# New cost numbers for the list scheduler that orders a Gated DeltaNet layer's front

## The chip, the cores and the metric

The kernel runs on one core of a Trainium2 chip. The core has TensorE for matrix products (PE in the profile, its weight loads PEld), VectorE (DVE), ScalarE (ACT), GpSimd (POOL), SyncE (SP), which here issues the transfers, and 16 DMA engines behind a hardware queue. Each engine works through its own list of instructions in order, and semaphores connect the lists. The metric is device time in microseconds of one execution, the median of several runs.

## The reference

One layer of a diffusion backbone in fp32: a bidirectional gated DeltaNet over 512 latent tokens with a prefix of 256 context tokens, width 1024, 8 heads of 128, then a mixture of 16 experts with expert-choice routing. Both are fed by RMSNorm and modulation (shift, scale, gate) that is computed from `c`. Cut to what matters here:

```
mod = silu(c) @ w_mod + b_mod                    # 6 x 1024 columns: shift, scale, gate of both parts
u = modulate(rmsnorm(x), shift, scale)           # latent and context tokens
q, k, v = silu(short_conv(u @ w_in, width 5)); z = u @ w_z
decay g and beta from u; l2norm of q and k
for both directions, for each head, in chunks of 64 tokens:
    L = I + strict_lower((beta k) k^T * decay)   # 64 x 64, unit lower triangular
    u_vals, w_keys = solve(L, [beta v, beta k exp(gcum)])
    scan over chunks:  v_new = u - w S;  o = q_dec S + att v_new;  S = g S + k_tail^T v_new
y = (rmsnorm(o) * gain * silu(z)) @ w_out
x = x + gate * y
then: 16 experts, each takes its best tokens; out = x + gate * sum(p * (silu(h Wg) * (h Wu)) Wd)
```

## The kernel before

The kernel has a **front** (norms, projections, eight heads, output projection, router) and then a **loop over the experts**, which gathers tokens by a one-hot matmul (L1511, tile `gc`) and multiplies them with the experts' weights (L1561, L1580). Those weights, tiles `w`, come in transfers of 1 to 2 MB that SP issues (L636) as soon as buffers are free, the first of them while the front still runs.

A product in fp32 is made of three matmuls on split operands: `wh` and `uh` are the rounded halves, `wl` and `ul` the remainders (L141 to L143 for the projections, L457 to L459 for the output projection, "a triple" below). ACT rounds, and DVE or POOL subtracts (L299 and L303 for the projections' weights, loaded as `wt` on L136; L733 and L735 for the output weights).

**The heads.** Each head q goes through steps that follow on one another:

- convolutions of its projected columns (L283, DVE);
- part A, `head_a`: two loads `ff` of the decay rows (L1060, from `grow_d`), a mask on POOL (L1065), exponentials on ACT, products into `ct` and `cd` on DVE (L1116 to L1125), and `cd` goes to DRAM (`bd`, L1128);
- the inversion of the triangular blocks: `lb` comes back from `bd` in another layout (L1137), POOL works 62 alternating steps on 96 partitions (L1148 `tb`, L1150 `xb`), and the result goes out as `xd` (L1153) and returns as `cr` (L1158);
- part B, `head_b`: from `cx` (L1217, DVE) to the transposed inverse `XT` (L1277, L1278);
- the scan over chunks in two directions (L1302 to L1352: `R` L1318, `Vs` L1326, `vx` L1330, the state L1337), with a decayed query `qa`, which is loaded (L1290), exponentiated on ACT and multiplied on POOL (L1298);
- norm and gating, transposes on PE (L1382), the head's output `ot` (L1385).

**The modulations.** 32 pieces of 512 KB (`mods` and `mod_piece`, L338 to L398) yield shift, scale and gate columns that are needed late. A string names the engine of each piece; a piece on DVE is 8 operations (L373, L375), then one matmul (L396) and one addition (L398). Loads are planned 7 us apart from 50 us on, into two buffers. The last eight pieces are the columns of the gate row `gtm`.

**The output projection.** `out_w` scales a piece of the output weights with `gtm` on POOL (L723; the code makes it wait for all eight columns), rounds it (L733) and subtracts (L735). Pieces come through a ring of three buffers `wot` (L716). Then 64 triples in five groups of heads, (0,1), (2,3), (4,5), (6) and (7), go to PE, and DVE adds each result to `hres` (L475). L766 splits the heads' outputs. The router follows: transposes L537, logits L514, L524, and L578.

**What sets the order.** Nothing of the front is written in the order in which it is issued. Every step is a Python generator that yields `Ask(engine, duration, earliest time, slot)` in front of each operation, and `run` (L213 to L237) is a greedy list scheduler: it keeps a planned time at which each engine is free, takes the step that can start first, or within a window (`LOOK`) one of better rank on the same engine, emits its instruction, and moves the planned time on by the duration. The result of a step counts as available after its duration and the hand-over `HOP` of its engine, or 0.06 us on the same engine. `dma` plans transfers as one queue with a rate and a latency. `RANK` is 1 for the scan and part A, 4 for part B, 5 and 6 for output, 7 for mods and convolutions. So the numbers in the `Ask`s decide in which sequence each engine's list is written; on the chip the lists run in order, as their semaphores allow.

## Time and profile before

| | us |
|---|---|
| median of three runs | 1574.02 (1568.37 to 1576.02) |
| the profiled execution | 1573.24 |
| its span | 1571.5 |
| PE, DVE, ACT, POOL busy | 1374.7, 721.5, 405.3, 381.0 |
| first gather of the expert loop | 633.51 |

The profile gives, for one execution, what each engine did at which time. A row of the timeline is an operation (or several alike): its start, its duration, engine, line, result and operands, and in brackets how long the engine had been idle and what ended the wait. A row of the groups sums operations of one line and shape. A row of the waits sums the idle time of an engine by what it waited for. A row of the windows shows how long each engine worked in a stretch of time, the granted share of TensorE's full clock, the busy share of the DMA engines and what they moved.

### The profile page before, as it was taken

Reading aid. Unit: us, or ns where it says so; the run is one execution under the profiler, and the core shown is the slowest. Engines: PE = TensorE matmul, PEld = TensorE weight load, DVE = VectorE, ACT = ScalarE, POOL = GpSimd, SP = SyncE. Lnnn points to the kernel's source line nnn. Section 1 sums busy time; section 2 is a strip of 40 time slices with the busy share of each in tenths; the row PEclk is TensorE's granted clock in tenths of the full one; section 3 lists DMA queues with packets and bytes.
Section 4 is the critical chain, followed back from the end, with each engine's and each line's share of the span. In section 5 each row is a group of like instructions: output and inputs, shape, how many; then the busy total and the mean of one; then the engine's idle time right before and its main releaser. Section 6 shows DMA issues by size and latency. Waiting matters only on the chain.

```text
span 1571.5 us, 20699 instructions
## 1 busy us (share of the span) xinstructions
PE 1374.7 (87%) x8058; PEld 752.6 (48%) x8058; DVE 721.5 (46%) x1545; ACT 405.3 (26%) x1038; POOL 381.0 (24%) x645
## 2 busy tenths in 40 slices
PE   5889898988986889999999989889889899899867
PEld 1677687766875766433434324224223323324314
DVE  7779896977995896222222222222222222222103
ACT  3356474655574533000000000000000000000012
POOL 2548866857657830000000000000000000000001
PEclk8889999999998999999999999999999999999979
DMA  8145443443453566899999999999999999999992
GB/s 347 54 135 142 135 114 91 117 130 95 133 122 72 205 243 248 364 426 426 425 426 425 425 426 426 427 425 425 426 425 426 426 425 426 425 426 426 425 426 109
DMA packets 112515, 480.12 MB, mean 306 GB/s; under 512 B 45505, under 2 KB 66209, under 8 KB 81826
## 3 DMA queue, kind: packets, MB, share of 16 engines
q1 hardware_dynamic: 112418, 478.81, 77.9%
q8 instruction: 63, 1.03, 0.3%
q14 instruction: 34, 0.28, 0.1%
HBM read 471.92 MB, written 6.86 MB: 305 GB/s over the span
## 4 chain that ended last, share of the span: by engine, by line
DMA 48%; PE 26%; DVE 14%; POOL 8%; issue 2%; ACT 1%; SPq 0%; DVEq 0%; POOLq 0%; ACTq 0%
DMA w<-in_wgu 25%; DMA w<-in_wd 13%; PE gu L1580 10%; PE dn L1561 4%; POOL xb L1150 3%; POOL tb L1148 3%; DMA cr<-xd 2%; DVE e L375 2%; PE gc L1561 2%; PE gc L1511 2%; DMA fg<-in_fg 1%; DVE wl L303 1%; DMA ff__690<-grow_d 1%; DMA ff__1139<-grow_d 1%; PE gc L1548 1%
## 5 line engine op out<-in xcount | busy, mean ns | idle before, releaser
L1580 PE MATMUL gu<-w,xsT 128*64 128x512 f32 x2044 | 472.9, 606 | 32.4 <-DMA w<-in_wgu 31.6
L1580 PEld LDWEIGHTS gu<-w,xsT 128*64 128x64 f32 x2044 | 138.4, 138 | 291.5 <-issue 239.4
L1667 POOL TENSOR_TENSOR hres<-acc,fg 128x256 f32<-128x256 f32 (+1 forms) x6 | 6.0, 1004 | 953.1 <-DVE acc L1655 953.0
L1561 PE MATMUL dn<-w,work 128*64 128x512 f32 x896 | 202.0, 600 | 25.2 <-DMA w<-in_wd 25.2
L1550 DVE TENSOR_TENSOR acc<-gc,acc 128x512 f32<-128x512 f32 x104 | 70.7, 690 | 299.5 <-PE gc L1548 299.5
L141 PE MATMUL pp<-uh,wh 128*128 128x512 f32 (+1 forms) x368 | 153.4, 417 | 1.7 <-ACT cz L265 1.7
L143 PE MATMUL pp<-uh,wl 128*128 128x512 f32 (+1 forms) x368 | 138.9, 377 | 3.8 <-DVE wl L303 2.9
L142 PE MATMUL pp<-ul,wh 128*128 128x512 f32 (+1 forms) x368 | 137.9, 375 | 0.0
L1561 PEld LDWEIGHTS dn<-w,work 128*64 128x64 f32 x896 | 62.4, 137 | 154.2 <-issue 116.8
L1148 POOL TENSOR_TENSOR tb<-lb,xb 96x126 f32<-96x126 f32 (+22 forms) x248 | 118.3, 477 | 65.8 <-DMA lb<-bd 48.6
L1150 POOL TENSOR_TENSOR xb<-xb,tb 96x126 f32<-96x126 f32 (+22 forms) x248 | 125.1, 504 | 19.4
L1532 ACT ACTIVATE work<-tr 128x512 f32<-128x512 f32 x14 | 8.4, 597 | 423.1 <-PE tr L1525 423.1
L1512 DVE TENSOR_SCALAR xsT<-gc,ffn 128x128 f32<-128x128 f32 x64 | 26.2, 410 | 154.1 <-PE gc L1511 154.1
L1542 ACT CAST yh<-work 64x512 fp32r<-64x512 f32 x28 | 17.3, 617 | 253.1 <-DVE work L1539 252.8
L143 PEld LDWEIGHTS pp<-uh,wl 128*128 128x128 f32 x368 | 74.7, 203 | 16.1 <-DVE wl L303 3.3
L141 PEld LDWEIGHTS pp<-uh,wh 128*128 128x128 f32 x368 | 75.1, 204 | 10.7 <-ACT cz L265 2.2
L142 PEld LDWEIGHTS pp<-ul,wh 128*128 128x128 f32 x368 | 75.3, 205 | 6.3
L1511 PEld LDWEIGHTS gc<-oneh,hres 128*128 128x128 f32 x512 | 64.5, 191 | 20.2 <-issue 18.3
L1511 PE MATMUL gc<-oneh,hres 128*128 128x128 f32 x512 | 69.2, 280 | 0.4 <-DVE oneh L1504 0.4
L375 DVE SCALAR_TENSOR_TENSOR e<-e,cs,e 128x128 f32<-128x128 f32 x133 | 66.0, 512 | 1.8
L1613 DVE TENSOR_TENSOR work<-gu,work 128x512 f32<-128x512 f32 x32 | 22.0, 692 | 80.9 <-PE gu L1580 79.7
L1548 PEld LDWEIGHTS gc<-yh,pgt 128*128 128x128 f32 x112 | 19.8, 186 | 82.0 <-issue 68.2
(443 smaller groups left out, 2042.7 us busy)
## 6 DMA issues: line engine op xcount, KB each, us to landing
w<-in_wgu SPq DMA_DIRECT2D x100, 2048.0 KB, 34.3
w<-in_wd SPq DMA_DIRECT2D x45, 2048.0 KB, 34.3
w<-in_wgu SPq DMA_DIRECT2D x55, 1024.0 KB, 31.9
w<-in_wd SPq DMA_DIRECT2D x22, 1024.0 KB, 31.8
e<-in_wm SPq DMA_DIRECT2D x32, 512.0 KB, 4.4
wt<-in_win SPq DMA_DIRECT2D x31, 512.0 KB, 4.6
w<-in_wdt SPq DMA_DIRECT2D x6, 2048.0 KB, 30.7
wm<-in_wm SPq DMA_DIRECT2D x3, 2048.0 KB, 14.6
```

Of the source, the lines that this page charges most:

```text
L141: pe.matmul(pp, wh[:, k, :], uh[i][:, k, :], start=k == 0, stop=False)
L142: pe.matmul(pp, wh[:, k, :], ul[i][:, k, :], start=False, stop=False)
L143: pe.matmul(pp, wl[:, k, :], uh[i][:, k, :], start=False, stop=k == KT - 1)
L375: v.scalar_tensor_tensor(acc, wm[:, k], cs1[:, k, 0:1], acc, op0=OP.mult, op1=OP.add)
L1148: g.tensor_tensor(t_, lb[:, k + 1:, k:k + 1].to_broadcast([2 * NB, m, n_]), xb[:, k:k + 1, 0:n_].to_broadcast([2 * NB, m, n_]), OP.mult)
L1150: g.tensor_tensor(xb[:, k + 1:, 0:n_], xb[:, k + 1:, 0:n_], t_, OP.subtract)
L1511: pe.matmul(pg, hres[:, t, k * P:k * P + P], oneh[:, t].rearrange("p a b -> p (a b)"), start=t == 0, stop=t == NC_LAT - 1)
L1512: v.tensor_scalar(xsT[:, k, :], pg, ffn[:, 0, k:k + 1], ffn[:, 1, k:k + 1], op0=OP.mult, op1=OP.add)
L1548: pe.matmul(pcb, pgt[:, t, :], yh[:, dh], start=True, stop=True)
L1550: v.tensor_add(acc[t // 2][:, t % 2, cs], pcb, hres[:, t, cs] if first else acc[t // 2][:, t % 2, cs])
L1561: pe.matmul(pd[64 * g_:64 * g_ + 64], hs_[g_][i][:, cb, 64 * j:64 * j + 64], wcols(w, c0, w_), start=ft == 0, stop=ft == 15, tile_position ...
L1580: pe.matmul(gu[m][f // 2][hs], xsT[:, k, es], wcols(w, 2048 * m + 512 * f, 512), start=k == 0, stop=k == KT - 1, tile_position=(0, 64 * (f ...
```

## The change

Only numbers that the list scheduler works with are changed: about 60 durations, the hand-overs, and the plan for transfers. No operation is added, removed or changed, and ranks, the engines of the mod pieces, the planned times of their loads and the window are as before. The hand-over behind PE falls from 0.27 to 0.22 us, behind ACT and DVE from 0.33 to 0.06, behind POOL from 0.35 to 0.08; many durations rise. A transfer is planned with 0.3 us at its start, 380 GB/s and 1.3 us of latency, and three kinds get an extra latency of their own (`more`): the loads `ff` 4.5, the loads for `qa` 3.5, `cr` 1.3 us. The diff, cut to the parts of the scheduler itself and one or two lines of each kind of step:

```diff
--- before.py
+++ after.py
...
-    HOP = {"P": 0.27, "A": 0.33, "V": 0.33, "G": 0.35, "D": 0.0, None: 0.0}
+    HOP = {"P": 0.22, "A": 0.06, "V": 0.06, "G": 0.08, "D": 0.0, None: 0.0}
     PRE = 1
     E_AT = (410, 425)
...
     LOOK = {"P": 0, "A": 0.75, "V": 0.5, "G": 0, "D": 0.25}
     dq = [2.0]
 
-    def dma(nbytes, at=0.0):
-
-        dq[0] = max(dq[0], at + 0.7) + nbytes / 360e3
-        return dq[0] + 1.1
+    def dma(nbytes, at=0.0, more=0.0):
+
+        dq[0] = max(dq[0], at + 0.3) + nbytes / 380e3 + more
+        return dq[0] + 1.3
...
-    av = lambda n_: 0.1 + n_ * 0.00084
-    dv = lambda n_: 0.08 + n_ * 0.00104
+    av = lambda n_: 0.14 + n_ * 0.00088
+    dv = lambda n_: 0.15 + n_ * 0.00104
...
-                    t = yield Ask("A", 0.59, t)
+                    t = yield Ask("A", 0.69, t)
...
-                t = yield Ask("V", 0.25, t)
+                t = yield Ask("V", 0.42, t)
...
-        t = yield Ask("P", 0.15, t + 3.0, "pq")
+        t = yield Ask("P", 0.11, t + 3.0, "pq")
...
-                    t = yield Ask("P", 0.67, lambda: fin(*((w_, h) for h in hs for w_ in (f"wow{hf}", "woo"))), "pp" if h == hs[0] else None)
+                    t = yield Ask("P", 0.69, lambda: fin(*((w_, h) for h in hs for w_ in (f"wow{hf}", "woo"))), "pp" if h == hs[0] else None)
...
-        t = yield Ask("P", 0.85, lambda: fin(("w7", 0), ("O", nh - 1), *(("lg", i) for i in range(NC_LAT))), "pq")
+        t = yield Ask("P", 0.44, lambda: fin(("w7", 0), ("O", nh - 1), *(("lg", i) for i in range(NC_LAT))), "pq")
...
-        t = yield Ask("G", 1.25, lambda: None if fin(*(("M", j) for j in range(8))) is None else max(t, *(done["M", j] for j in range(8))))
+        t = yield Ask("G", 1.31, lambda: None if fin(*(("M", j) for j in range(8))) is None else max(t, *(done["M", j] for j in range(8))))
...
-        t = yield Ask("V", 4.3, t)
+        t = yield Ask("V", 6.0, t)
...
-            tf = dma(3 << 17, tf)
+            tf = dma(3 << 17, tf, 4.5)
...
-            t = yield Ask("P", 0.225, t, f"sc{d}")
+            t = yield Ask("P", 0.11, t, f"sc{d}")
...
-                t = yield Ask("A", 0.25, t)
+                t = yield Ask("A", 0.365, t)
```

How the lists change is shown at three places.

SP, from the store of the decay rows `grow_d` to the store `bd` of head 0; `wt` are weight loads of the projections and `e` loads of the mods. Before:

```order
L1022 DMA grow_d<-gr 96x128
L344 DMA e_454<-in_wm 128x1024
L1060 DMA ff__660<-grow_d 128x6x128
L1060 DMA ff__690<-grow_d 128x6x128
L136 DMA wt<-in_win 128x1024
L344 DMA e_454<-in_wm 128x1024 x2
L136 DMA wt<-in_win 128x1024
L1128 DMA bd_849<-cd 128x12x32
```

SP, the same place after:

```order
L344 DMA e_449<-in_wm 128x1024
L136 DMA wt<-in_win 128x1024
L1060 DMA ff__704<-grow_d 128x6x128
L136 DMA wt<-in_win 128x1024
L344 DMA e_449<-in_wm 128x1024
L1060 DMA ff__776<-grow_d 128x6x128
L344 DMA e_449<-in_wm 128x1024
L136 DMA wt<-in_win 128x1024
```

The two loads of head 0, next to one another before, now have a weight load ahead of the first, and another and a mod load between them.

POOL, in the middle of head 7's inversion before (`tb`, `xb`), with three of the scalings of output weights by the gate row (`wot<-wot,gtm`):

```order
L1148 TENSOR_TENSOR tb<-lb,xb 96x110
L1150 TENSOR_TENSOR xb<-xb,tb 96x10x11
L723 TENSOR_TENSOR wot<-wot,gtm 128x512 x3
L1148 TENSOR_TENSOR tb<-lb,xb 96x108
L1150 TENSOR_TENSOR xb<-xb,tb 96x9x12
```

POOL, from the end of the same inversion after:

```order
L1148 TENSOR_TENSOR tb<-lb,xb 96x16
L1150 TENSOR_TENSOR xb<-xb,tb 96x16
L1298 TENSOR_TENSOR qa<-qa,wa 128x512
L355 TENSOR_TENSOR e_449<-e_449,cs_117 128x512 x2
L364 TENSOR_TENSOR e_449<-e_449 128x512
L364 TENSOR_TENSOR e_449<-e_449 128x256
L367 TENSOR_TENSOR e_450<-e_449 128x128
L723 TENSOR_TENSOR wot<-wot,gtm 128x512 x3
L723 TENSOR_TENSOR e_449<-e_449,gtm 128x512 x2
L723 TENSOR_TENSOR wot<-wot,gtm 128x512 x11
```

All 16 scalings now stand behind the last inversion and behind a last mod piece on POOL (L355 to L367); eight of them stood within it before.

DVE, around the last head's output `ot` before (`lg`, `hT` belong to the router, `hres<-pp,hres` adds a result of the output projection):

```order
L475 TENSOR_TENSOR hres<-pp,hres 128x512
L1368 TENSOR_SCALAR m<-m 128x4
L1369 SCALAR_TENSOR_TENSOR m<-ssq,m 128x4
L539 COPY hT<-pq 128x512
L1385 SCALAR_TENSOR_TENSOR ot<-pq,og,wa 128x512
L527 COPY lg<-pq 128x16
L539 COPY hT<-pq 128x512
L766 TENSOR_TENSOR ol<-ot,oh 128x512
```

DVE, the same place after:

```order
L375 SCALAR_TENSOR_TENSOR e_450<-e_449,cs_117,e_450 128x128 x5
L1385 SCALAR_TENSOR_TENSOR ot<-pq,og,wa 128x512
L375 SCALAR_TENSOR_TENSOR e_450<-e_449,cs_117,e_450 128x128
L398 TENSOR_TENSOR gtm<-pq,gtm 128x128
L735 TENSOR_TENSOR wol<-wot,woh 128x512 x2
L766 TENSOR_TENSOR ol<-e_449,oh 128x512
L735 TENSOR_TENSOR wol<-wot,woh 128x512
L766 TENSOR_TENSOR ol<-e_449,oh 128x512
```

The last gate column (L375, L398) now stands behind `ot`, and with it every subtraction of output weights (16 L735) and every addition to `hres` (40 L475; 8 stood there before). On PE all 64 triples follow the last head's transposes, where 8 did.

## Rows read from the trace of the kernel before

**Rows 1.** Windows: stretch, its length, busy us (operations) by engine, clock, DMA share, GB/s.

```profile
103.50:557.30 453.80, 389.43 (x3098) 326.19 (x3096) 372.77 (x822) 267.35 (x742) 320.99 (x583) 0.93 0.47 123
557.30:605.80 48.50, 43.35 (x420) 35.50 (x418) 40.40 (x94) 15.85 (x46) 8.49 (x7) 1.00 0.73 284
605.80:633.50 27.70, 25.88 (x127) 14.88 (x127) 19.49 (x57) 9.06 (x19) 0.00 (x0) 1.00 0.43 167
...
700.00:877.00 177.00, 174.16 (x838) 68.06 (x834) 47.64 (x96) 11.44 (x21) 0.00 (x0) 1.00 1.01 426
```

**Rows 2.** Timeline: start us, duration us, engine, line, out<-in; head 7 and the tail.

```profile
550.58 0.33 SPq L1153 DMA_DIRECT2D xd<-xb  x1
...
557.34 0.33 DVE L1217 COPY cx<-cr 128x96 f32<-128x96 f32 x2 [0.69 <-DMA cr<-xd]
...
605.79 0.75 DVE L1385 SCALAR_TENSOR_TENSOR ot<-pq,og,wa 128x512 f32<-128x512 f32 x1 [1.62 <-PE pq L1382]
...
613.40 0.40 PE L457 MATMUL pp<-woh,oh 128*128 128x512 f32 x1
613.63 0.39 PE L458 MATMUL pp<-woh,ol 128*128 128x512 f32 x1
...
615.61 0.39 PE L459 MATMUL pp<-wol,oh 128*128 128x512 f32 x1
...
633.51 1.74 PE L1511 MATMUL gc<-oneh,hres 128*128 128x128 f32 x8 [0.44 <-DVE oneh L1504]
```

**Rows 3.** Waits of POOL from 60 to 640 us: total us, times, longest us.

```profile
POOL tb L1148 <- DMA lb<-bd: 48.6, 7, 12.4
POOL qa L1298 <- ACT qa L105: 21.1, 7, 10.2
...
POOL wot L723 <- DMA wot<-in_wo: 16.6, 5, 6.9
```

**Rows 4.** Timeline of SP's queue around head 0's loads.

```profile
80.13 0.54 SPq L1060 DMA_DIRECT2D ff__690<-grow_d  x1
...
100.27 0.33 SPq L136 DMA_DIRECT2D wt<-in_win  x1
```

**Rows 5.** Groups of DVE and POOL before 640 us: count, busy us, mean ns, idle before.

```profile
L375 DVE SCALAR_TENSOR_TENSOR e<-e,cs,e 128x128 f32<-128x128 f32 x133 | 66.0, 512 | 1.8
...
L283 DVE SCALAR_TENSOR_TENSOR cv<-pad,cw,cv 128x772 f32<-128x772 f32 x32 | 37.4, 1169 | 2.2 <-ACT cv L281 1.9
...
L475 DVE TENSOR_TENSOR hres<-pp,hres 128x512 f32<-128x512 f32 x40 | 27.3, 686 | 7.3 <-PE pp L459 7.0
...
L735 DVE TENSOR_TENSOR wol<-wot,woh 128x512 fp32r<-128x512 f32 x14 | 13.1, 946 | 0.0
...
L723 POOL TENSOR_TENSOR wot<-wot,gtm 128x512 f32<-128x512 f32 x14 | 18.4, 1329 | 22.7 <-DMA wot<-in_wo 16.6 <-DVE hres L475 4.9 <-PE sc L1333 1.3
```

**Rows 6.** Timeline of POOL ahead of the inversions of heads 6 and 7.

```profile
437.69 1.29 POOL L1298 TENSOR_TENSOR qa<-qa,wa 128x512 f32<-128x512 f32 x1 [10.23 <-ACT qa L105]
...
451.32 0.81 POOL L1148 TENSOR_TENSOR tb<-lb,xb 96x31 f32<-96x31 f32 x1 [8.57 <-DMA lb<-bd]
...
499.27 1.26 POOL L1298 TENSOR_TENSOR qa<-qa,e 128x512 f32<-128x512 f32 x1 [4.39 <-ACT qa L105]
...
506.01 0.25 POOL L1148 TENSOR_TENSOR tb<-lb,xb 96x31 f32<-96x31 f32 x1 [0.78 <-DMA lb<-bd]
```

**Rows 7.** Group of PE from 560 to 640 us.

```profile
L537 PE MATMUL pq<-ident,hres 128*128 128x128 f32 x32 | 4.9, 276 | 0.1
```

**Rows 8.** POOL's inversion: two steps alike; then L1150's group in head 6, in head 7.

```profile
397.64 0.43 POOL L1148 TENSOR_TENSOR tb<-lb,xb 96x126 f32<-96x126 f32 x1
...
401.29 1.28 POOL L1148 TENSOR_TENSOR tb<-lb,xb 96x126 f32<-96x126 f32 x1
...
L1150 POOL TENSOR_TENSOR xb<-xb,tb 96x126 f32<-96x126 f32 (+22 forms) x31 | 17.4, 561 | 2.4
...
L1150 POOL TENSOR_TENSOR xb<-xb,tb 96x126 f32<-96x126 f32 (+22 forms) x31 | 14.6, 472 | 2.4
```

More of the change, by code (lines that the diff above doesn't have):

```diff
@@ L407, in first_projections @@
                 for i in range(2):
-                    t = yield Ask("P", ((0.45, 0.24), (0.67, 0.36))[j][i] * (1 if k > 2 else 1.5), lambda: None if ("w", j - 2) not in done or ("u", k) not in done else max(done["w", j - 2], done["u", k]), None if k else tags[j][i])
+                    t = yield Ask("P", ((0.46, 0.24), (0.70, 0.36))[j][i] * (1 if k > 2 else 1.5), lambda: None if ("w", j - 2) not in done or ("u", k) not in done else max(done["w", j - 2], done["u", k]), None if k else tags[j][i])
                     if k == 0:
@@ L434, in bulk @@
                 for k in range(KT):
-                    t = yield Ask("P", (0.67, 0.36)[i], both, None if k else "pp")
+                    t = yield Ask("P", (0.69, 0.355)[i], both, None if k else "pp")
                     if k == 0:
@@ L497, in route_c @@
         done["rw", 0] = t
-        t = yield Ask("P", 0.22, t, "pq")
+        t = yield Ask("P", 0.1, t, "pq")
         sl = take("pq")
@@ L515, in with_router @@
         give(sl2, t)
-        t = yield Ask("A", 0.2, t, "rs")
+        t = yield Ask("A", 0.27, t, "rs")
         sl3 = take("rs")
@@ L520, in with_router @@
         give(sl, t)
-        t = yield Ask("P", 0.22, t, "pq")
+        t = yield Ask("P", 0.1, t, "pq")
         sl = take("pq")
@@ L525, in with_router @@
         give(sl3, t)
-        t = yield Ask("V", 0.13, t)
+        t = yield Ask("V", 0.165, t)
         v.tensor_copy(dst, pc)
@@ L865, in mod_first @@
             give(sl, t)
-            t = yield Ask("P", 0.2, t, "pq")
+            t = yield Ask("P", 0.4, t, "pq")
             sl = take("pq")
             pc = mod_cols(ms, 2 * nk)
-            t = yield Ask("V", 0.7, t)
+            t = yield Ask("V", 0.76, t)
             k2 = slice(k0, k0 + nk)
@@ L965, in gates @@
         give(psl[0, 1], t)
-        t = yield Ask("V", 1.0, t)
+        t = yield Ask("V", 1.6, t)
         v.tensor_copy(trir, tri[:, 0])
@@ L1012, in gates @@
         give(sl, t)
-        t2 = yield Ask("P", 0.2, t, "pq")
+        t2 = yield Ask("P", 0.08, t, "pq")
         sl = take("pq")
@@ L1180, in head_t @@
         done["T", h] = ta
-        t = yield Ask("P", 0.43, t, "pq")
+        t = yield Ask("P", 0.36, t, "pq")
         sl = take("pq")
         pt = tr4(qT, range(2, 6))
-        t = yield Ask("A", 1.0, t)
+        t = yield Ask("A", 0.77, t)
         junk = ga.tile([P, P], F32, tag="junk", bufs=1, name="junk")
@@ L1219, in head_b @@
         tx = t
-        t = yield Ask("P", 0.85, t, "pq")
+        t = yield Ask("P", 0.25, t, "pq")
         sl = take("pq")
@@ L1231, in head_b @@
         give(sl, t)
-        t1 = yield Ask("P", 0.85, t, "pq")
+        t1 = yield Ask("P", 0.25, t, "pq")
         sl1 = take("pq")
@@ L1247, in head_b @@
         give(sl1, t1)
-        t2 = yield Ask("A", 1.0, t2)
+        t2 = yield Ask("A", 1.48, t2)
         for b in range(4):
@@ L1263, in head_b @@
         give(sl, t)
-        t3 = yield Ask("V", 0.7, tx)
+        t3 = yield Ask("V", 1.3, tx)
         for b in range(4):
             v.tensor_copy(XT[0][R[b], :, R[b]], cx[R[b], 0, 1])
-        t4 = yield Ask("A", 1.0, tx)
+        t4 = yield Ask("A", 1.44, tx)
         for b in range(4):
             s.copy(XT[1][R[b], :, R[b]], cx[R[b], 1, 1])
-        t = yield Ask("P", 0.95, max(t, t2, t3, t4), "pq")
+        t = yield Ask("P", 0.4, max(t, t2, t3, t4), "pq")
         sl = take("pq")
@@ L1291, in decay_q @@
             x["qd"].append(qd)
-            t0.append(dma(1 << 18, t))
+            t0.append(dma(1 << 18, t, 3.5))
         for d in range(2):
```

102 lines of the change are left out of this document (51 added, 51 removed).

## The prediction

> **What bounds the kernel now.** I read the windows first, to find where a microsecond counts. From the first gather on the DMA engines are the bound: between 700 and 877 us their share is 1.01 and the transfers never pause [rows 1]. That part is a stream of fixed size. Before it the front ends at the first gather, 633.51 us [rows 2], and in its last 27.7 us the DMA share is only 0.43 [rows 1]: the weight buffers are full and the stream stands. So a microsecond won or lost at the first gather is one won or lost at the end, and only the front has to be forecast.
>
> In the front no engine is full. Between the end of the first head's part A and head 7's first step of part B (103.5 to 557.3 us) PE is busy 389 of 454 us, DVE 373, POOL 321 [rows 1]: 82% for DVE, 81 us idle. What holds them is the chain of heads: part A on DVE, `bd` and `lb` by DMA, 62 inversion steps on POOL, `xd` and `cr` by DMA, part B on DVE, scan. The waits of POOL show that chain: 48.6 us for `lb`, then 21.1 us for the exponentials of `qa` and 16.6 us for `wot` [rows 3]. Its last piece is what the rest must wait for: head 7's `cx` at 557.34, its `ot` at 605.79, the last of the output matmuls at 615.61, the first gather at 633.51 [rows 2]. So the tail is 27.7 us: 9.8 with only 8 of 64 triples left, and 17.9 for routing.
>
> **The change part by part.** No instruction comes or goes; what moves is order. I go through it in the sequence of that chain.
>
> *Head 0.* SP now has a weight load `wt` ahead of the first `ff` load and a second `wt` and a mod load ahead of the second. Before, the `ff` load stood at 80.13 and the second `wt` could issue only at 100.27 [rows 4], so `ff__776` may come up to 20 us later; with its affine step following its landing, I take 12 to 16 us for the end of head 0's part A. DVE has 19 us more work in front of that point: 8 convolutions (L283, 1.17 us each), 13 steps of mods (L375, 0.51 each) and 2 splits (L303) [rows 5]. I cost it at nothing because this work covers it; without the cover it is 12 to 16 us on every later head.
>
> *DVE up to head 7's part B.* In front of head 7's `cx` now stand 11 fewer adds of L475, 8 fewer of L735 and 14 fewer of L375: 11 x 0.686 + 8 x 0.946 + 14 x 0.512 = 22.3 us [rows 5]. Other small operations (5 of L766 and 5 of L398 leave, some routing comes) make it about 24. The cumulated DVE work in front of the earlier heads' `cx` is within 7 us of before up to head 5, apart from head 0: the gain is made in heads 6 and 7. If every idle microsecond stays, `cx` comes 22 us earlier (the durations overlap a little in the busy time); if idle shrinks with work, 24/0.82 = 29. I take 29, so 528 us, since the waits in the last two gaps before inversions [rows 6] are of the kind that shrinks when DVE brings `cd` earlier.
>
> *POOL.* Eight L723 stood between the steps of head 7's inversion; now all 16 stand behind it: 8 x 1.33 = 10.6 us [rows 5] out of an inversion that ran from 506.01 [rows 6] to 550.58, when `xd` was issued [rows 2]. That is why POOL can follow the 29 us. What is late next there is `lb`. Against it, both L1298 of another head now stand in front of six of the seven later inversions; before, it was so in the gaps ahead of heads 6 and 7, where POOL waited 10.23 us and 4.39 us for the first of the two exponentials [rows 6]. In the forecast I cost this at nothing, since the engine waited for `lb` in the same gaps anyway (8.57 us behind the 10.23); the other end of the range is a rival below.
>
> *From `cx` to `ot` of head 7.* In front of the last `ot` there are now 45 us less of DVE work, 21 of them between `cx` and `ot`: the adds and splits of the output projection. The stretch took 48.5 us with DVE busy 40.4 [rows 1]. If all of those 21 us were on the path it becomes 28, if none, it stays; the scan also waits in turn for PE and ACT, so I take 37 (ends 28 and 45). `ot` then ends at 528 + 37 = 565, 41 earlier.
>
> *The tail.* What left the front is now behind `ot`. On PE 64 triples follow the last transposes, where 8 did; a triple takes 0.69 us (three matmuls, 0.23 from one start to the next [rows 2]). They cannot start at once. The output weights are scaled by a gate row that needs all eight of its columns, and the last one is now finished on DVE behind `ot`: one L375, 0.51, and one of L398 with PE's step between them, by estimate 2.6 us; then the first five L723 on POOL, 5 x 1.33 = 6.65; then rounding on ACT and L735 on DVE (0.95), about 1.5: 11 us. Then PE has 64 x 0.69 = 44.2 us of triples and 40 transposes of L537 (4.9 us for 32 in the old order, so 6.1 [rows 7]), and with some 2 of the router's small matmuls: 52 us. DVE has 40 adds of L475, 16 of L735 and 8 of L766 beside this, 27 + 15 + 6 = 48, just under it. Then routing, 17.9 as now. Sum 11 + 52 + 17.9 = 81.
>
> One more cost is in the tail: `wot` has three buffers and eleven more loads than buffers can hold, all issued on SP between weight loads of 1 to 2 MB. POOL already waited 16.6 us in five places for `wot` [rows 3], but hidden. A buffer is needed every third slice, 3 x 2.76 = 8.3 us; POOL, ACT and DVE hold it for 3, which leaves 5 for the load. I take 4 us in all, between 0 and 20. The tail is 85 us instead of 27.7: +57.
>
> Sum: -29 - 12 + 57 = +16 at the first gather, on the profiled execution's 1573.2 us (0.8 under the median of 1574.0): **1590 us**.
>
> **A rule against the change.** On POOL the same step of 96x126 elements took 0.43 us at 397.64 and 1.28 us at 401.29, when DVE ran a convolution and a split with two operands; the L1150 half of an inversion took 14.6 us for head 7 and 17.4 for head 6 [rows 8]. The Trainium skill (GPSIMD Engine Reference, Key points) says why that could be: GpSimd shares its SBUF interfaces with VectorE and meets contention from DVE instructions with two SBUF inputs. The trace agrees. By that rule a denser DVE is partly paid for by POOL; what it would do here is rival D.
>
> **The rivals.** *A, faster.* The chain closes up: DVE loses half of its 81 us of idle besides the 24 of work. Then `cx` of head 7 comes at 493 to 500, `ot` at 534, and -72 + 57 = -15: 1558. For it: the new numbers are close to the traced durations, so waits that the list did not foresee may go. Against: DVE work in front of heads 1 to 5 is unchanged, and SP makes head 0 later.
>
> *B, slower, and more than forecast.* POOL is in order, so an L1298 that waits for its exponential holds the inversion behind it. Before, that cost 14.6 us in two gaps [rows 6]; four more gaps at the 7.3 of their mean are 29, and with 6 in 10 of it on the path 17: 1607. It decides from the point where `qa` lands later than `lb`.
>
> *C, the same.* Gain and loss cancel: with `ot` 57 us earlier (at 549) the first gather stays at 633. That needs `cx` at 518 and 31 us from there to `ot`, both inside my bounds. 1574. The change not doing what it says, new numbers with no effect on the order, is excluded by the order; effect without result is this case.
>
> *D, slower.* Convolutions and mods that moved into the idle time lie beside inversions. If four of the eight inversions go from head 7's level to head 6's, 2.8 us in L1150 and by estimate as much in L1148, that is 4 x 5.6 = 22, half of it on the path: 1601.
>
> **How the numbers follow.** Forecast 0.43, A 0.17, B 0.11, C 0.20, D 0.09. The forecast's own range comes from its unknowns: 22 to 36 us for `cx`, 28 to 45 for the way to `ot`, 0 to 20 for `wot`: 1575 to 1610. With A on one side and B and D on the other, 8 in 10 lie from 1562 to 1612. A measurement here can tell some 0.5%, 7.9 us, from no change. Slower by more: most of the forecast and all of B and D, 0.61. Within: C and the forecast's lower edge, 0.22. Faster: 0.17.
>
> **What would show it.** In the profile after: head 7's `cx` near 528 and `ot` near 565; no L723 inside an inversion; first triple 8 to 14 us behind `ot` and all 64 in a row on PE at full clock; the first gather near 650, 80 to 90 behind `ot`. A is seen by `ot` under 545; B by POOL waits for `qa` of 40 us or more; D by L1150 and L1148 of over 255 us in sum; `wot` by POOL's waits in front of L723 behind `ot`. I am wrong if the tail is well under 75 us, or if `cx` has not moved by 20.

## The result, and the profile after

The changed kernel takes 1658.7 us (median of four runs, 1654.7 to 1664.6) against 1573.0 for the kernel before: a ratio of 1.0551, interval 1.0509 to 1.0593. It is slower, as forecast, but by 86 us where 16 were forecast, and far outside the range. Nearly all of it lies in the front, as the argument had it: the first gather comes at 717.58 us instead of 633.51 [rows 2], 84 us later, and behind it the stream is as long as before.

The timeline of the kernel after, the rows that answer to [rows 2] (start, duration, engine, line, out<-in, idle before and what ended it):

```profile
573.32 0.33 SPq L1153 DMA_DIRECT2D xd<-xb  x1
...
580.81 0.33 DVE L1217 COPY cx<-cr 128x96 f32<-128x96 f32 x2 [0.31 <-DMA cr<-xd]
...
618.90 0.75 DVE L1385 SCALAR_TENSOR_TENSOR ot<-pq,og,wa 128x512 f32<-128x512 f32 x1 [0.56 <-PE pq L1382]
...
627.70 0.80 PE L457 MATMUL pp<-woh,oh 128*128 128x512 f32 x1 [6.95 <-ACT woh L733]
...
688.02 0.48 PE L457 MATMUL pp<-woh,oh 128*128 128x512 f32 x1
...
717.58 1.74 PE L1511 MATMUL gc<-oneh,hres 128*128 128x128 f32 x8 [0.44 <-DVE oneh L1504]
```

Head 7's `cx` is 23 us later than before, where 29 us earlier were forecast. From `cx` to `ot` it takes 38.1 us (37 forecast, 48.5 before). From `ot` to the first gather it takes 98.7 us (85 forecast, 27.7 before). So the step on the way to `cx` is the one that failed, by 53 us, and the tail was taken 14 us too short.

Two windows show what became of the work that left the front (columns as in [rows 1]). The kernel before, from 60 us to its last `ot`:

```profile
60.00:605.79 545.79, 465.40 (x3667) 390.55 (x3666) 443.82 (x956) 303.29 (x840) 353.97 (x610) 0.93 0.48 137
```

The kernel after, the same and its tail:

```profile
60.00:618.90 558.90, 452.91 (x3415) 377.10 (x3415) 406.26 (x893) 288.90 (x809) 315.72 (x592) 0.87 0.37 100
618.90:717.58 98.68, 78.91 (x377) 54.37 (x378) 67.39 (x120) 25.83 (x48) 24.24 (x17) 0.87 0.61 235
```

The third column of busy times is DVE: 38 us of its work did leave the front (443.8 to 406.3), and 13 us were added to the stretch all the same. DVE's idle time there went from 102 to 153 us. The waits show where it idles now. DVE before, the longest (us in total, times, longest):

```profile
DVE cx L1217 <- DMA cr<-xd: 23.2, 7, 6.4
DVE vx L1330 <- ACT Vs L1326: 12.0, 18, 1.7
```

DVE after:

```profile
DVE R L1318 <- PE sc L1315: 24.4, 51, 1.8
DVE wa L1337 <- PE sc L1333: 18.0, 43, 0.9
DVE wl L303 <- ACT wh L299: 14.7, 8, 3.8
DVE vx L1330 <- ACT Vs L1326: 13.7, 23, 1.9
```

Before, DVE came to `cx` ahead of `cr` and waited there, on the chain of heads. After, it waits half a microsecond at a time between the steps of a scan, and at seven of the eight heads it comes to `cx` when `cr` has already landed, 0.1 to 8.1 us before: the 0.31 us at head 7 are all the waiting for `cr` that is left. The landing of `cr` itself came later too; why is told below, under the ring of heads.

### The profile page after: what moved, and what is told of

Its sections match the earlier page's. It is cut to its first block, busy times and chain, and to the rows that moved or that the text cites. A ratio compares the mean times of both kernels' runs of the same rounds, so it can differ in the third digit from the quotient of the medians.

```text
span 1656.1 us, 20778 instructions
## 1 busy us (share of the span) xinstructions
PE 1412.3 (85%) x8058; PEld 776.7 (47%) x8058; DVE 733.3 (44%) x1545; ACT 408.5 (25%) x1038; POOL 363.9 (22%) x645
## 4 chain that ended last, share of the span: by engine, by line
PE 39%; DMA 39%; DVE 10%; issue 4%; ACT 4%; POOL 3%; SPq 0%; DVEq 0%; ACTq 0%; POOLq 0%
DMA w<-in_wgu 24%; DMA w<-in_wd 12%; PE gu L1580 10%; PE dn L1561 3%; PE pp L141 3%; PE pp L143 2%; PE pp L142 2%; PE gc L1561 2%; PE sc L1333 2%; PE gc L1511 1%; DMA fg<-in_fg 1%; PE sc L1321 1%; POOL xb L1150 1%; PE sc L1315 1%; DMA wt<-in_win 1%
## 5 line engine op out<-in xcount | busy, mean ns | idle before, releaser
L141 PE MATMUL pp<-uh,wh 128*128 128x512 f32 (+1 forms) x368 | 147.1, 400 | 10.0 <-ACT wh L299 7.1
L1150 POOL TENSOR_TENSOR xb<-xb,tb 96x126 f32<-96x126 f32 (+22 forms) x248 | 111.5, 449 | 19.4
L1148 POOL TENSOR_TENSOR tb<-lb,xb 96x126 f32<-96x126 f32 (+22 forms) x248 | 104.8, 423 | 47.4 <-DMA lb<-bd 29.6
L1548 PE MATMUL gc<-yh,pgt 128*128 128x512 f32 x112 | 52.3, 487 | 7.7 <-DVE acc L1550 7.7
L1326 ACT ACTIVATE Vs<-sc,vsc 128x128 f32<-128x128 f32 x80 | 27.9, 366 | 122.7 <-PE sc L1321 122.2
```

The costliest lines, as they stand in the source:

```text
L141: pe.matmul(pp, wh[:, k, :], uh[i][:, k, :], start=k == 0, stop=False)
L1148: g.tensor_tensor(t_, lb[:, k + 1:, k:k + 1].to_broadcast([2 * NB, m, n_]), xb[:, k:k + 1, 0:n_].to_broadcast([2 * NB, m, n_]), OP.mult)
L1150: g.tensor_tensor(xb[:, k + 1:, 0:n_], xb[:, k + 1:, 0:n_], t_, OP.subtract)
L1326: s.mul(Vs, pv, x["vsc"][:, d, c:c + 1])
L1548: pe.matmul(pcb, pgt[:, t, :], yh[:, dh], start=True, stop=True)
```

## What was tried

Fifteen kernels, each timed beside the kernel before on the same chip. The table puts together what their profiles show: how many of the 64 triples stand behind the last head's transposes, when the last `ot` starts, and the tail from there to the first gather (us). Behind each measured time below stand its ratio to the kernel before and, after the comma, the 95% interval of that ratio.

| kernel | triples behind | last `ot` | tail | first gather | ratio of times |
|---|---|---|---|---|---|
| before | 8 | 605.8 | 27.7 | 633.5 | 1 |
| after | 64 | 618.9 | 98.7 | 717.6 | 1.055 |
| e1 durations | 64 | 605.6 | 110.1 | 715.7 | 1.047 |
| e2 hand-over, transfers | 33 | 610.9 | 57.5 | 668.4 | 1.024 |
| e3 old hand-over | 64 | 606.9 | 87.1 | 694.1 | 1.038 |
| e4 mods at rank 5 | 8 | 697.9 | 28.8 | 726.6 | 1.055 |
| e5 hand-over | 8 | 632.1 | 29.2 | 661.3 | 1.018 |
| e6 transfers | 8 | 611.4 | 28.3 | 639.7 | 1.003 |
| e7 old DVE durations | 8 | 651.2 | 29.0 | 680.2 | 1.030 |
| e8 PE durations | 53 | 595.1 | 73.9 | 669.1 | 1.022 |
| e9 mods left out | 8 | 602.5 | 27.7 | 630.2 | 0.995 |
| e10 PE, mods at rank 6 | 8 | 636.5 | 29.7 | 666.1 | 1.022 |
| e11 scan's PE | 36 | 604.4 | 61.4 | 665.8 | 1.019 |
| e12 rank 6 | 8 | 626.6 | 28.2 | 654.8 | 1.015 |
| e13 short inversion | 8 | 586.6 | 27.7 | 614.3 | 0.987 |
| e14 scalings behind | 17 | 600.6 | 45.7 | 646.3 | 1.009 |
| e15 no gate wait | 64 | 619.5 | 110.2 | 729.7 | 1.062 |

### Which part of the change does it

**e1**: the durations of the change alone.

```diff
-    av = lambda n_: 0.1 + n_ * 0.00084
-    dv = lambda n_: 0.08 + n_ * 0.00104
+    av = lambda n_: 0.14 + n_ * 0.00088
+    dv = lambda n_: 0.15 + n_ * 0.00104
...
-                t = yield Ask("V", 0.25, t)
+                t = yield Ask("V", 0.42, t)
```

> The kernel before with the new durations alone; hand-overs and the plan for transfers stay old. Theory (two causes): the longer DVE durations fill the planned DVE, so the mods (last in rank) and with them the gate row come last: all 64 triples stand behind the last transposes, and the tail from the last `ot` to the first gather is 90 to 105 us (27.7 before, 98.7 with the whole change). But the old hand-overs keep the planned scan at 3.2 us a chunk, near the 3.1 to 3.8 of the trace, so POOL's waits for `qa` stay under 40 us (21 before, 77 after) and the last `ot` is at 575 to 600. Sum 1610 to 1640. Rival (durations alone do it all): `ot` near 619 as well, 1655.

Measured: 1653.2 us (1.0471, 1.0426 to 1.0516). The triples and the tail are as the theory said, or worse (110.1), but `ot` stood at 605.6, not at 575 to 600: 64 us less of DVE work in front of it than before (380.1 us busy instead of 443.8) and not a microsecond earlier. So the durations alone make nearly the whole loss, all of it in the tail, and the theory's gain in front is gone. The total is the rival's 1655, but not by the rival's path: that had `ot` near 619.

**e2**: the hand-overs and the plan for transfers, without the durations.

```diff
-    HOP = {"P": 0.27, "A": 0.33, "V": 0.33, "G": 0.35, "D": 0.0, None: 0.0}
+    HOP = {"P": 0.22, "A": 0.06, "V": 0.06, "G": 0.08, "D": 0.0, None: 0.0}
...
-            tf = dma(3 << 17, tf)
+            tf = dma(3 << 17, tf, 4.5)
```

> The whole change but for the durations, which are the old ones: new hand-overs and new plan for transfers. Theory: 33 triples stand behind the last transposes, so the tail is 50 to 65 us; the planned scan takes 2.3 us a chunk, so loads of `qa` and their products stand too early in their lists: POOL waits for `qa` 50 us or more, and the last `ot` comes at 610 to 630. Sum 1600 to 1625. Rival (the waits come from the durations): POOL waits for `qa` under 30 us, `ot` under 590, sum under 1580.

Measured: 1614.2 us (1.024, 1.0189 to 1.0292), `ot` 610.9, tail 57.5, POOL's waits for `qa` 80.1: as the theory had it in every number. That its reason was wrong came out with the next run.

**e3**: the whole change with the old hand-overs.

```diff
-    HOP = {"P": 0.22, "A": 0.06, "V": 0.06, "G": 0.08, "D": 0.0, None: 0.0}
+    HOP = {"P": 0.27, "A": 0.33, "V": 0.33, "G": 0.35, "D": 0.0, None: 0.0}
```

> The whole change but for the hand-overs, which are the old 0.27, 0.33, 0.33, 0.35 us. Theory: the planned scan is back at 3.2 us a chunk, so POOL's waits for `qa` fall from 77 to 20 to 40 us and the last `ot` comes at 580 to 600 instead of 619; the tail stays at 90 to 100, since 64 triples stand behind the last transposes as in the whole change. Sum 1620 to 1645. Rival (the extra latencies of the transfer plan make the waits): waits of 60 us or more, `ot` near 619, 1655 to 1665.

Measured: 1635.4 us (1.0377, 1.0347 to 1.0407). The waits for `qa` did not fall to 20 to 40, they rose:

```profile
POOL qa L1298 <- ACT qa L105: 113.2, 12, 25.2
```

and with 113 us of them `ot` comes at 606.9, 12 us earlier than after the whole change with its 77. So these waits do not come from the hand-overs, and their sum does not tell how late `ot` is. What tells is where they stand. In e3 none of them stands between the steps of an inversion. After the whole change two L1298 stand in the middle of head 7's, and POOL waits there for 13.6 us, on the way to `xd`:

```profile
556.10 0.29 POOL L1150 TENSOR_TENSOR xb<-xb,tb 96x56 f32<-96x56 f32 x1
569.96 1.26 POOL L1298 TENSOR_TENSOR qa<-qa,wa 128x512 f32<-128x512 f32 x1 [13.57 <-ACT qa L105]
571.18 0.31 POOL L1148 TENSOR_TENSOR tb<-lb,xb 96x45 f32<-96x45 f32 x1
```

Behind it the steps run on to the issue of `xd` at 573.32 and to `cx` at 580.81 with hardly a wait. Another 2.6 us stand inside head 0's inversion. The rest of the 77 us lies in the gaps between inversions, and there it did cost little: the inversions of heads 0 to 5 and 7 still start within 0.4 us of the landing of `lb`, only head 6's starts 4.3 us behind it. So rival B came true in one place. No run takes this wait alone out of the changed kernel; its price of up to 13 us is read from the trace, and agrees with the 12 us that e3 is earlier.

**e5** and **e6**: the hand-overs alone, and the plan for transfers alone (the two pieces of the diff of e2, one each).

> The kernel before with the new hand-overs alone. 8 triples stand behind the last transposes and head 0's loads go out about as before. Theory as it stands after the first runs (a ring over two heads, from the transposed inverse of head q-2 to that of head q, sets the last `ot`, whatever DVE work stands in front; the durations set the tail): the ring keeps its 106 to 122 us a pair, so the last `ot` at 600 to 620 and the tail 27 to 35 us: 1565 to 1595. Rival (short hand-overs slow the scan and so the chain): `ot` later than 625, over 1595.

> The kernel before with the new plan for transfers alone. Head 0's second load stands behind a weight load, as with the whole change. Theory: head 0's `cd` moves from 106 to 115 to 120 us, the ring carries 10 to 20 us of that to the last `ot` (610 to 625), the tail stays at 27 to 35, since 8 triples are left: 1575 to 1600. Rival (a head that starts late is caught up in the gaps of the inversions): `ot` at 600 to 608, 1565 to 1578.

Measured: e5 1602.7 us (1.0179, 1.0143 to 1.0215), `ot` at 632.1, which is the rival's time: short hand-overs alone cost 26 us in the chain. The rival's reason, a slow scan, is not what the trace shows: the end of part B of head 6 is only 3.6 us later than before (523.5 for 519.9), and most of the loss comes at head 7's `cd` (521.4 for 483.8). e6 1579.6 us (1.0026, 1.0007 to 1.0046), `ot` 611.4: within half a percent. `cd` of head 0 came 5 us later where 9 to 14 were expected; at the end of part B the kernel is 9 us late at head 0 and still 9 us late at head 7.

**e7** and **e8**: the whole change with the old DVE durations, and the kernel before with the new PE durations alone.

```diff
-                t = yield Ask("V", 0.335, t)
+                t = yield Ask("V", 0.26, t)
```

> The whole change, but the durations of DVE's operations are the old ones. 8 triples are left behind the last transposes. Theory: the new DVE durations are what puts the mods and with them the gate row last; with the old ones the tail is 28 to 40 us instead of 99, while head 0's loads are as late as with the whole change, so the last `ot` comes at 610 to 635: 1580 to 1610. Rival (the tail's work only moves in front of `ot` and delays it by as much, as with the mods at rank 5): `ot` beyond 660, over 1630.

```diff
-            t = yield Ask("P", 0.225, t, f"sc{d}")
+            t = yield Ask("P", 0.11, t, f"sc{d}")
```

> The kernel before with the new durations of PE's operations alone. 53 triples are left behind the last transposes instead of 8. Theory: PE durations alone leave the tail: 80 to 95 us; the last `ot` does not come earlier for the work that left the front, so 595 to 610: 1620 to 1645. Rival (the work that leaves the front brings `ot` forward, as the prediction had it): `ot` at 580 or earlier, 1610 or less.

Measured: e7 1622.3 us (1.0296, 1.0263 to 1.0329). The tail is 29.0, as the theory said, but `ot` comes at 651: between theory and rival, nearer to the rival. e8 1610.4 us (1.0215, 1.0181 to 1.025), `ot` 595.1 and a tail of 73.9: PE's shorter durations alone make a long tail, though a shorter one than the theory's 80 to 95, and `ot` came 11 us earlier, with 29 us less of DVE work in front. The total is the rival's 1610, but `ot` is far from its 580.

**e11**: of these, only the four of the scan's matmuls.

> The kernel before with four numbers changed: the durations of the scan's matmuls on PE, 0.225 to 0.11 (three of them) and 0.45 to 0.22. 36 triples are left behind the last transposes. Theory: a shorter planned PE is enough to push the output projection behind the last head: tail 52 to 65 us, `ot` 592 to 610, 1590 to 1620. Rival (it takes the durations of DVE as well): tail under 40 us, under 1585.

Measured: 1604.6 us (1.0187, 1.0159 to 1.0215), `ot` 604.4, tail 61.4: as the theory had it. Four numbers suffice to push 28 triples behind the last head.

### Whether the work in front sets the last output

**e9**: the order and all planned numbers of the kernel before, but seven of the eight operations of each mod piece on DVE are not issued.

```diff
-                else:
+                elif k < 1:
                     v.scalar_tensor_tensor(acc, wm[:, k], cs1[:, k, 0:1], acc, op0=OP.mult, op1=OP.add)
```

> The kernel before, order and planned numbers unchanged, but of each mod piece on DVE only the first of eight operations is issued; the 133 operations of L375 (66 us of DVE work, all in front of the last `ot`) are left out, and with them seven eighths of those modulations' sums. Theory (the ring of heads sets the last `ot`): DVE's idle time in front of `ot` grows by 45 us or more, `ot` moves from 606 to 590 to 606, the tail stays at 28: 1555 to 1576. Rival (the prediction's premise, work in front divided by DVE's share): `ot` 60 to 80 us earlier, under 550, and 1500 to 1515.

Measured: 1568.8 us (0.9948, 0.9922 to 0.9974). The window of this kernel from 60 us to its last `ot`:

```profile
60.00:602.48 542.48, 462.89 (x3664) 391.96 (x3662) 388.86 (x822) 302.43 (x839) 350.88 (x609) 0.92 0.49 138
```

DVE is busy 55 us less than before (443.82), and the stretch is 3.3 us shorter. This run bears on the prediction's first term: dividing the work that leaves the front by DVE's share gives 55/0.82 = 67 us here, and it was worth 3. The work left out is spread over all heads and is not the same operations as those that the change moved, so it is a test of the rule, not of the change's own 24 us.

**e13**: as much work taken from POOL, out of the inversions: 12 of 62 steps.

```diff
-            t_ = tb[:, :m * n_].rearrange("p (i j) -> p i j", i=m)
+            t_ = tb[:, :m * n_].rearrange("p (i j) -> p i j", i=m); tt_ = (lambda *z: None) if 12 <= k < 18 else g.tensor_tensor
-            g.tensor_tensor(t_, lb[:, k + 1:, k:k + 1].to_broadcast([2 * NB, m, n_]),
+            tt_(t_, lb[:, k + 1:, k:k + 1].to_broadcast([2 * NB, m, n_]),
...
```

> The kernel before, order and planned numbers unchanged, but POOL leaves out 12 of the 62 steps of each inversion (six of its 31 rounds): 96 operations, some 54 us of POOL's busy time and 61 with the gaps, about as much as the mods left out on DVE, which moved the last `ot` by 3 us. Theory (the ring of heads sets the last `ot`; four inversions of 7.7 us less lie on its chain of heads 1, 3, 5, 7): `ot` 25 to 45 us earlier, 560 to 581, tail 28 as before: 1530 to 1550. Rival (neither engine's work counts, only the waits between): less than 12 us earlier.

Measured: 1554.8 us (0.9871, 0.9836 to 0.9906).

```profile
60.00:586.55 526.55, 455.66 (x3664) 384.04 (x3662) 441.72 (x956) 302.59 (x839) 303.13 (x513) 0.95 0.52 142
```

POOL is busy 51 us less (353.97 before), and `ot` comes 19 us earlier: less than the 25 to 45 expected, and five to six times what about as much work on DVE was worth (the time is just outside the theory's 1530 to 1550). So work of the inversions is largely on the chain, and the mods on DVE hardly are. The inversions became shorter by less than what was taken out, 42.8 to 39.3 us in the mean of heads 2 to 7, and a part of that is given back as waiting: POOL's waits for `lb` rose from 48.6 [rows 3] to 53.1 us.

### What sets the tail

**e4**: the whole change, the mods at rank 5.

```diff
-    RANK = {"S": 1, "O": 6, "A": 1, "add": 2, "I": 6, "mod": 7,
+    RANK = {"S": 1, "O": 6, "A": 1, "add": 2, "I": 6, "mod": 5,
```

> The whole change, with the rank of the mods 5 instead of 7, so that they are planned earlier; 8 triples stand behind the last transposes, as in the kernel before. Theory: the tail goes back to 27 to 35 us, a gain of some 65; the chain of heads keeps its fault (waits for `qa` of 60 us or more) and has the mods, the weights' splits and the adds in front of the last `ot` again, so that one comes at 620 to 650. Sum 1590 to 1625. Rival (the mods' place is all that is wrong): `ot` at 606 or earlier, 1575 or less.

Measured: 1663.1 us (1.0547, 1.0508 to 1.0586). The tail is 28.8, as the theory said; `ot` is at 697.9, beyond both. The mods now stand ahead of the convolutions (rank 7) and `cd` of head 3 comes at 357 us instead of 255. Ahead of the chain, they cost as much as behind it.

**e10** and **e12**: the mods at rank 6, with the new PE durations and in the kernel before.

> The kernel before with the new PE durations and the rank of the mods 6 instead of 7; 8 triples are left behind the last transposes (53 with the PE durations alone, where `ot` came at 595 and the tail took 74 us). Theory: the tail goes back to 28 us, and the 50 us of DVE and POOL work that return to the front delay `ot` by at most their own length less the idle time they fill: `ot` at 600 to 630, 1565 to 1600. If `ot` stayed at 595, this would beat the kernel before: 1563. Rival (work in front costs as much as it saves behind): `ot` at 640 or later, 1610.

> The kernel before with one number changed that belongs to none of the change's parts, the rank of the mods, 6 instead of 7. 8 triples are left, as before. Theory: the order before is a favourable one among its neighbours; a change of any number reorders all heads, and the ring catches most of it: `ot` at 605 to 635, tail 28 to 30, 1572 to 1605. Rival (only the numbers of this change do harm): within 0.5% of the kernel before.

Measured: e10 1609.7 us (1.0222, 1.0186 to 1.0259), `ot` at 636.5, at the edge between theory and rival. e12 1598.2 us (1.0149, 1.0117 to 1.0181): one number that the change doesn't touch, and `ot` is 21 us later.

**e14**: one part of the change that the prediction counted on, alone: rank 5 for the inversion keeps the lists up to head 7's inversion and puts the scalings L723 behind it.

```diff
-"I": 6, "mod": 7,
+"I": 5, "mod": 7,
```

> The kernel before with one number changed, the rank of the inversion, 5 instead of 6. The lists are those of before up to head 7's inversion; then the scalings of output weights (L723) stand behind it instead of within it, and 17 triples instead of 8 stand behind the last transposes. Theory: that inversion takes 33 to 36 us instead of 44.6, the last `ot` comes 7 to 12 us earlier, the tail grows by 5 to 9 us for nine more triples: 1566 to 1577. Rival: the scalings come too late for the output projection and the tail grows by 20 us or more: over 1580.

Measured: 1591.2 us (1.0088, 1.0059 to 1.0117). Head 7's inversion took 30.0 us instead of 44.6, even better than said, but `ot` came only 5.2 us earlier: `cx` follows `xd` by 13.1 us, before 6.8. And nine more triples behind the transposes made the tail 18 us longer. The rival is right.

**e15**: the whole change, with L723 multiplying each weight by itself instead of by the gate row.

```diff
-        t = yield Ask("G", 1.31, lambda: None if fin(*(("M", j) for j in range(8))) is None else max(t, *(done["M", j] for j in range(8))))
-        g.tensor_mul(wt, wt, gtm[:, 512 * hf:512 * hf + 512])
+        t = yield Ask("G", 1.31, t)
+        g.tensor_mul(wt, wt, wt)
```

> The whole change, but L723 multiplies each weight by itself instead of by the gate row and so waits for no mod; the gate is left out of the output. Seven of the 16 scalings then stand ahead of or within the last inversion; 64 triples still stand behind the last transposes, since the splits of the heads' outputs (L766) rank as low. Theory: the tail loses the wait for the last gate column and the first scalings, 6 to 9 us, and a part of the waits for `wot`: 80 to 90 us instead of 99; the last `ot` is at 610 to 625. Sum 1640 to 1655. Rival (the tail is made by the gate): tail under 60, under 1625.

Measured: 1673.2 us (1.0622, 1.0581 to 1.0662); `ot` 619.5, tail 110.2. Neither theory nor rival: without any gate to wait for the tail is longer. So the late gate row alone does not make the tail; why the tail became longer without that wait isn't shown. In the table the tail goes with the count of triples behind, and with the splits and adds that stand there with them: 28 to 30 us with 8, 46 with 17, 58 with 33, 61 with 36, 74 with 53, 87 to 110 with 64, so 1.0 to 1.5 us for each triple beyond the eight, from 33 on, where a triple takes PE 0.69 us [rows 2]. No run moves the triples alone, so that they set the tail rests on this order of the kernels.

None of the fifteen beats the kernel before without leaving work out.

## Why the prediction was right or wrong

**Head 0.** "I cost it at nothing because this work covers it" was wrong. The second load landed at 99 us, and the convolutions of the head's own keys `ck`, which the exponentials in front of `ct` need too, ended only at 98.5 (76.9 before). Then the covering work itself was late. Timeline of DVE, POOL and SP after:

```profile
111.74 0.34 DVE L375 SCALAR_TENSOR_TENSOR e<-e,cs,e 128x128 f32<-128x128 f32 x1
112.00 0.68 DVE L1116 TENSOR_TENSOR ct<-ff__704,ff__776 128x512 f32<-128x512 f32 x1
...
116.67 0.38 DVE L1125 STREAM_TRANSPOSE cd<-cd 128x192 f32<-128x192 f32 x1
...
117.50 0.72 SPq L1060 DMA_DIRECT2D ff__1049<-grow_d  x1
...
122.61 1.50 SPq L1137 DMA_DIRECT2D lb<-bd  x2
...
125.27 1.46 POOL L1065 TENSOR_SCALAR_AFFINE_SELECT ff__1049<-ff__1049 128x768 f32<-128x768 f32 x1 [25.35 <-DMA ff__1049<-grow_d]
...
134.63 0.25 POOL L1148 TENSOR_TENSOR tb<-lb,xb 96x31 f32<-96x31 f32 x1 [1.50 <-DMA lb<-bd]
```

ACT came to the exponentials of head 0 at 108.86 us (96.71 before), mods and convolutions stood ahead of `ct` on DVE until 112 us, `cd` came 10.5 us later than before, and then head 1's `ff` load and the loads of `qa` went out between `bd` and `lb`, whose landing POOL waited for until 134.63, 20 us later than before. At the end of part B the first two heads are 18 and 25 us late. What covers a load must not stand in front of what follows the load.

**The ring of heads.** The term "24/0.82 = 29" is the step that failed. It had two companions that were put at nothing: the loads of head 0, and the waits for `qa` on POOL. From the end of part B of head q-2 to that of head q, the mean over heads 2 to 7 in us (the inversion goes from its first step on POOL to the issue of `xd` on SP):

| | part A | `bd`, `lb` | inversion | `xd`, `cr`, until `cx` | part B | sum |
|---|---|---|---|---|---|---|
| before | 30.9 | 13.1 | 42.8 | 8.0 | 18.8 | 113.7 |
| after | 36.3 | 9.7 | 37.9 | 13.8 | 16.0 | 113.6 |
| e9, less DVE work | 30.8 | 13.7 | 41.9 | 8.2 | 17.6 | 112.1 |
| e13, less POOL work | 30.0 | 12.1 | 39.3 | 8.8 | 19.0 | 109.2 |

The inversions and part B are indeed shorter by 8 us, and the waits for `lb` fell from 48.6 [rows 3] to 29.6. But part A became longer by 5.4 us and the way from `xd` to `cx` by 5.8, and these took it all back. The trace shows where.

On the way to `cx` it is mostly the list of SP, which issues transfers in order. The steps of the inversion, first to last, fell from 42.8 to 35.1 us, but SP issued `xd` 2.8 us behind the last step (at once before), and `cr` 6.2 us behind `xd` (2.4 before); the landing took as long as before (5.2 us, 5.6), and DVE came to `cx` 2.5 us after it. At head 6 SP stood at two loads of `qa`, and issued `xd` 8 us after the last step:

```profile
508.96 0.22 POOL L1150 TENSOR_TENSOR xb<-xb,tb 96x16 f32<-96x16 f32 x1
...
513.48 3.52 SPq L1290 DMA_DIRECT2D qa<-grow_d  x2
517.09 0.45 SPq L1153 DMA_DIRECT2D xd<-xb  x1
...
523.45 0.36 SPq L1158 DMA_DIRECT2D cr<-xd  x1
```

SP's waits say what it stood for, from 60 to 620 us after. A load of a mod piece (L344) needs a buffer that DVE's L375 must free (37.4 us of waits before), and a load of `qa` (L1290) one that the scan's L1348 on PE must free:

```profile
SPq L344 <- DVE e L375: 122.4, 12, 27.3
SPq L1290 <- PE po L1348: 65.6, 9, 24.8
```

In part A, PE transposes the head's keys (L1042) 18.4 us behind the end of the earlier head's part B, 12.2 before. At heads 2, 3, 6 and 7 the keys had been ready for 29 to 90 us, and the transposes stood in PE's list behind steps of the scan, as at head 2 (PE after):

```profile
218.67 0.39 PE L1333 MATMUL sc<-Vs,ktok 128*128 128x128 f32 x2
218.90 0.60 PE L1042 MATMUL pq<-ident,ck 128*128 128x128 f32 x4
```

So the ring did not become shorter, and the lateness of the first heads was not won back: at the end of part B the heads 0 to 7 are 18, 25, 28, 31, 35, 35, 23 and 20 us late. The prediction had named this chain as the bound and had then costed it by the amount of work on an engine that is idle 18% of the time on it; e9 puts that work's price at 0.06 us for each us, where the sum had used 1.2. In place of 29 us earlier `cx` came 23 us later: its way led through the lists of SP, PE and POOL, and the waits in front of its steps there were not in the sum. What holds part A at 31 us when DVE has less to do wasn't tried, and what each of these delays is worth by itself is open: no run takes out one of them alone.

**POOL.** That L723 would leave the inversion, and be worth 10.6 us there, was right (inversion of head 7 in e14: 30.0 for 44.6); that the chain would follow was not (5.2 us). In the changed kernel itself head 7's inversion still took 42.3 us, because the wait of 13.57 us for `qa` stood in it where the scalings had been.

**From `cx` to `ot`** the time was right, 38.1 for 37, but partly by luck. DVE had 17 us less to do there (23.18 us for 40.39), not the 21 said, and the stretch became 10.4 us shorter; and PE ran it at a granted clock of 0.68 (1.00 before), which the forecast didn't have.

**The tail** had the right form and 85 for 98.7 us. The first triple came 8.8 us behind `ot` (11 said). The triples with the router's work took 60 us (52 and 4 for `wot` said) and what follows 29.6 (17.9). Three things were missing. PE waited much in the first part of the tail (busy 7.4 of 18 us from 620 to 638), and the granted clock there was 0.50, the lower of its two levels (1.2 and 2.4 GHz), where it had been 1.00 from 605 to 615 and was 0.99 again from 638 on. Windows after, the first column of busy times is PE:

```profile
605.00:615.00 10.00, 7.76 (x54) 6.62 (x54) 5.78 (x21) 1.77 (x7) 0.00 (x0) 1.00 0.32 107
620.00:638.00 18.00, 7.35 (x17) 5.18 (x18) 14.40 (x13) 5.89 (x10) 12.45 (x8) 0.50 0.60 205
638.00:645.00 7.00, 7.00 (x32) 5.68 (x31) 3.08 (x5) 0.00 (x0) 0.00 (x0) 0.99 0.97 400
```

The first triples ran at that level, 1.28 us apart; later ones are 0.69 apart. By these rows the four early ones cost some 2.4 us. The third product of the first triple also waited 3.7 us for its split `wol` (L459):

```profile
632.63 0.80 PE L459 MATMUL pp<-wol,oh 128*128 128x512 f32 x1 [3.71 <-DVE wol L735]
...
634.50 0.63 PE L457 MATMUL pp<-woh,oh 128*128 128x512 f32 x1
...
635.78 0.63 PE L457 MATMUL pp<-woh,oh 128*128 128x512 f32 x1
...
643.09 0.39 PE L457 MATMUL pp<-woh,oh 128*128 128x512 f32 x1
...
643.78 0.40 PE L457 MATMUL pp<-woh,oh 128*128 128x512 f32 x1
```

The largest is in what follows the triples. The last head's routing weights, done beside the scan before, now come last, with one copy on ACT behind four squares of `hres`, and the step of the router that needs them (L578) starts 9.2 us behind the last triple, where it was 0.2 us:

```profile
696.93 0.61 PE L524 MATMUL pq<-selr,rs 128*128 128x16 f32 x2 [5.01 <-ACT rs L519]
697.80 1.89 PE L578 MATMUL pq<-w,ot 128*128 128x16 f32 x8 [0.27 <-DVE w L527]
```

With these the tail is 98.7 us: the start 2.2 us shorter than said, the triples 4.3 longer, the end 11.7 longer. The wait for `wot` was there as said (29.0 us on POOL behind `ot`, 11.93 the longest), but most of it lies beside the triples.

**The rivals.** B's waits came, 77 us for the 40 asked. The prediction had put them at nothing because POOL waited for `lb` in the same gaps anyway, and for most of the gaps that held. It did not look for one inside an inversion: the 13.6 us at head 7, with 4.3 at head 6's start, are near B's 17 on the path. Rival C needed `cx` at 518, 39 us earlier, which lies outside the 22 to 36 that the prediction gave, though it calls it inside. D did not come: L1150 and L1148 took 216 us in sum, less than the 243 before. Between an inversion's first step and `xd` DVE spent 41.5 us on convolutions and 31.7 on mods, 68.0 and 55.1 before:

```profile
L1150 POOL TENSOR_TENSOR xb<-xb,tb 96x126 f32<-96x126 f32 (+22 forms) x248 | 111.5, 449 | 19.4
L1148 POOL TENSOR_TENSOR tb<-lb,xb 96x126 f32<-96x126 f32 (+22 forms) x248 | 104.8, 423 | 47.4 <-DMA lb<-bd 29.6
```

The rule of the Trainium skill (GPSIMD Engine Reference, Key points), that GpSimd meets contention from DVE instructions with two SBUF inputs, agrees with this: with fewer such DVE steps beside them, POOL's steps are 11% shorter. It has a limit here. The fast step at 397.64 [rows 8] also ran beside DVE instructions with two inputs, and there it was DVE that became slower (four took 2.00 us; one alone took 0.34, at 111.74 after). Beside the slow step at 401.29 the trace shows a split and a copy, and not the convolution that the prediction named. Timeline of DVE before:

```profile
396.73 2.00 DVE L375 SCALAR_TENSOR_TENSOR e<-e,cs,e 128x128 f32<-128x128 f32 x4
...
400.83 1.46 DVE L303 TENSOR_TENSOR wl<-wt,wh 128x1024 fp32r<-128x1024 f32 x1
```

The rule bore on the sum with the other sign than rival D gave it, and the 27 us less did not shorten the ring.

**Why more exact numbers made a worse list.** Shown is that each part that was tried alone does harm or next to nothing (e1, e5, e6, e8, e11; the durations of DVE, POOL and ACT were not tried alone), that the PE durations push the output projection behind the last head without any other number (e8, e11), and that DVE's do their part (e7: with the old ones, 8 triples are left). In the trace one of the scan's matmuls on PE is two instructions, and the next one starts 0.22 to 0.23 us after it (L1348 at 325.64, L1352 at 325.87 in the kernel after): that is the old number, and twice the new one, so that here the change was not a truer one. That the list with the old numbers is a favourable one among its neighbours, rather than a truer plan, has e12 for it, a single neighbour, and that none of the new orders beat it; how the durations starve the lowest ranks in the plan was only argued from the order.

## What to carry to other kernels

Before work is counted as gained because it leaves the front of a chain, take the same amount of work out of that engine and look (e9): where the chain is a ring of loads, transposes and waits through several engines, the work of an engine that is often idle may have next to no price there (3 us for 55), and moved behind the chain it can have its full one. For each step of the chain look at what stands in front of it in its list, and in the list that issues the transfers too: where a wait stands counts, not the sum of the waits. Numbers of a list scheduler are not measurements but settings: a truer number changes the whole order, so each is worth its run on the chip, and the count of instructions behind the last link of the chain (8 or 64 triples) told more of the result here than the work in front.
